# A hybrid decoder trunk: the output matrix w_out by seven half products, the first of them placed inside the output projection

## The chip, the core and the metric

The kernel runs on one core of one Trainium2 chip. The core has five engines that work side by side and meet at semaphores: TensorE (PE in the profile; PEld is its loading of the stationary operand), VectorE (DVE), ScalarE (ACT), GpSimd (POOL) and SyncE (SP), which here issues the transfers between the chip's main memory and the on-chip memory. TensorE writes its sums to banks of a separate memory (PSUM), from which VectorE and ScalarE read them. The metric is the device time of one execution in microseconds (us); the time of a kernel is the median of its runs.

## What is computed

Two layers of a decoder trunk over 512 tokens of width 1024, in float32. Each layer runs three mixers on the normed input, gates and merges them, projects the merge with `w_out`, and adds a feed-forward part:

```python
    xn = rmsnorm(x, norm1_g)
    proj = xn @ w_in
    ...
    y_ssd = ssd_mixer(...)
    y_mla = mla_mixer(...)
    y_gdn = gdn_mixer(...)
    gates = jax.nn.sigmoid(gate_logits.astype(jnp.float32)).astype(x.dtype)
    g_ssd, g_mla, g_gdn = jnp.split(gates, N_BRANCH, axis=-1)
    mixed = g_ssd * (y_ssd @ w_ssd_out) + g_mla * (y_mla @ w_mla_out) + g_gdn * (y_gdn @ w_gdn_out)
    h = x + mixed @ w_out
    f = jnp.square(jax.nn.relu(rmsnorm(h, norm2_g) @ w_up)) @ w_down
    return h + f
```

`w_ssd_out`, `w_mla_out`, `w_gdn_out` and `w_out` are 1024 x 1024, `w_up` is 1024 x 4096, `w_down` 4096 x 1024.

## The kernel before

**Float32 from three products.** Each operand of a large matmul is split into a rounded part "hi" and a remainder "lo" (`split_half`, lines 149 to 156: a copy on ScalarE at line 154, a subtraction on VectorE at line 155). `mm3` (lines 180 to 184) then issues three matmuls into one bank: hi·hi, hi·lo, lo·hi. Weights come in by SP as raw panels of 512 KB into two buffers `wraw` (line 161) and are split 512 columns at a time into a ring of four pairs `whi`, `wlo`. There are four accumulator banks ("acc"), three small ones ("sm") and one for transposes ("yt").

**Order of the work.** The program is written as straight Python; a scheduler places each instruction in its engine's queue by the program's order, its priority (`tc.high_priority()` moves instructions ahead) and its own estimate of when the inputs are there. On the chip each queue runs in the order that was so fixed. A pool is a stretch of on-chip memory whose tags each have one or more buffers ("slots"); a tile waits until the tile before it in the slot is released, and, for a pool opened where another was closed, until the tiles that lay at the same place are released (`reuse_waits="tile"`).

**Around the change.** The mixers live in the pool `br`, whose first tag is "tok" (five slots of 8 KB, among them v and the gate z of the two DeltaNet units). Each layer ends its mixers with two `gdn_unit` calls, which have a recurrent chain over four token blocks, and then `out_proj(w_gdn_out, 2, ...)` (lines 459 to 473), the projection of the third branch. It has four steps `dp`; each takes 256 of the 1024 output columns: 48 matmuls for two tiles of gate logits (from `xh`, `xl`, the normed input), a tanh on ScalarE into two "cva" buffers (line 464), then 48 matmuls with the branch's matrix, and on VectorE the multiplication by the gate (line 472) and the addition to the branches before (line 473), into eight tiles `mixed[d]`, one for each 128 columns, transposed so that columns lie on partitions and the 512 tokens along the row. (The gate's sigmoid is a tanh, so `mixed` holds twice the merge; the factor 0.5 comes later.)

Then `br` is closed, the residual h (4 tiles of 128 tokens, 2 MB) is loaded (line 1101), the eight `mixed` tiles are split to hi and lo (lines 250 and 251), and `w_out` runs as two column halves of 512 (`dense_T`): for each of the four token groups, all eight k, three matmuls of 128 x 128 by 512. The evacuation at line 1115 adds half the result to h, and ScalarE squares h for the norm (line 271). In the second half the token groups run one after the other; after the third, `norm_half(0)` scales tokens 0 to 255 by their norm (line 285), transposes them on TensorE (line 290) and splits them to `xh`, `xl` with the gain (lines 254 and 255), eight rows of 256 tokens. The other half of the tokens follows inside the first panel of `w_up`.

**The feed-forward part** takes four quarters `qd` of 1024 columns. `up` makes four panels of 256 columns of relu squared; after each panel it loads a block of `w_down` (`after(c)`, line 1201, 1024 KB each, in the order b11, b12, b22, b21), and after the third and fourth sums p1 = b11 + b12 and p3 = b12 + b22 on VectorE (line 1195). `down` multiplies by seven half products instead of eight (a Strassen form): the token halves, the row halves and the column halves make 2 x 2 blocks on each side, and seven products of sums of blocks (a11, a12, s2, s1, s3, s4, a22 with b11, b21, p2, p1, p3, b22, p4) give the four result blocks. Each product is 2 token groups x 4 k x 3 = 24 matmuls of 512 columns; VectorE adds each result to h (line 1236), makes p2 = p1 + b22 (line 1251) and p4 = p2 + b21 (line 1264). In the last quarter of layer 0 the norm of tokens 0 to 255 for layer 1 stands ahead of the last product a22, whose four k are then run token group by token group.

Of the kernel before, what the change touches and what calls it, by code (L numbers as in the profile page):

```python
# [10 lines left out]
F32 = mybir.dt.float32  # L11
# [44 lines left out]
def hybrid_kernel(ctx, tc, a, out, depth=2, taps=None):  # L56
# [294 lines left out]
    for ly in range(depth):  # L351
# [107 lines left out]
        def out_proj(w2d, br, yh, yl, pl, part=range(4), after=None):  # L459
            for dp in part:  # L460
                tg = []
                for ps in dense_F(weights(w_in, O_GATE + br * D + dp * 256, 256, D), tiles(256), D, xh, xl, after=after):
                    t_ = mk(pl, [P, S], F32, "cva", 2)
                    act.activation(t_, ps, AF.Tanh, scale=0.5)
                    tg.append(t_)
                for j, ps in enumerate(dense_F(weights(w2d, dp * 256, 256, D), tiles(256), D, yh, yl, after=after)):
                    d = 2 * dp + j
                    if mixed[d] is None:
                        mixed[d] = mk(lp, [P, S], F32, "mix", 8)
                        dve.scalar_tensor_tensor(mixed[d], tg[j], 1.0, ps, ALU.add, ALU.mult)  # L470
                    else:
                        dve.scalar_tensor_tensor(tg[j], tg[j], 1.0, ps, ALU.add, ALU.mult)
                        dve.tensor_tensor(mixed[d], mixed[d], tg[j], ALU.add)
# [619 lines left out]
        out_proj(a["w_gdn_out"][ly], 2, *yg, br)  # L1093
# [5 lines left out]
        h = mk(hpl, [P, T, D], F32, "h")  # L1099
        for t in range(T):  # L1100
            sync.dma_start(h[:, t, :], xsrc[t * P : (t + 1) * P, :])
        mh, mlo = hilo_tags(lp, "y")
        for d in range(KD):
            split_act(mh[d], mlo[d], mixed[d])
        last = ly == depth - 1
        hts = [h[:, t] for t in range(T)]
        ssq = [mk(sp, [P, 2], F32, "nss", 4) for _ in range(T)]
        xh, xl = hilo_tags(lp, "x")
        n2 = lambda i, pl, *tag: norm_half(i, hts, ssq, lambda k: col(g_n2 + k), pl, xh, xl, *tag)
        with tc.tile_pool(name="wo", bufs=1, reuse_waits="tile") as wo:  # L1110
            for c in range(2):

                def ev(t, ps):
                    hs_ = h[:, t, c * 512 : (c + 1) * 512]
                    dve.scalar_tensor_tensor(hs_, ps, 0.5, hs_, ALU.mult, ALU.add)
                    square(ssq[t][:, c : c + 1], hs_, wo, "hj")

                hold = list(zip(*hilo_tags(wo, "w"))) if c == 1 else None
                hook = (lambda t: t == 2 and n2(0, wo, "xr", 2)) if c == 1 else None
                dense_T(weights(a["w_out"][ly], c * 512, 512, D, hold), 512, D, mh, mlo, ev, hook=hook)  # L1120
# [16 lines left out]
        with tc.tile_pool(name="ff", bufs=1, reuse_waits="tile") as fp:  # L1137
# [51 lines left out]
            def down_weights(qd):  # L1189

                b = {}

                def plus(o, x, y):
                    for q in (slice(0, 1024), slice(1024, 2048)):
                        dve.tensor_tensor(o[:, q], x[:, q], y[:, q], ALU.add)

                def after(c):
                    i, j = ((0, 0), (0, 1), (1, 1), (1, 0))[c]
                    b[i, j] = mk(fp, [P, 4 * 512], F32, f"wr{i}{j}")
                    rows, cols = (slice(o + 512 * e, o + 512 * (e + 1)) for o, e in ((qd * D, i), (0, j)))  # L1200
                    sync.dma_start(b[i, j].rearrange("p (k n) -> p k n", k=4), a["w_down"][ly][rows, cols].rearrange("(k p) n -> p k n", p=P))
# [6 lines left out]
                return b, after  # L1208

            def down(qd, ops, b):  # L1210

                x, z = ([acc_bank() for _ in range(2)] for _ in range(2))

                def product(ps, n, raw, start, i, j, op, done):  # L1220

                    w = []
                    for k in range(4):
                        w.append(split_half(raw(k)))
                        if done == 2 and qd == 3:
                            continue
                        for t in range(2):
                            mul(ps, n, w, k, t, start)
                    for t in range(2):
                        if done == 2 and qd == 3:  # L1230
                            for k in range(4):
                                mul(ps, n, w, k, t, start)
                        r = 2 * i + t
                        hs_ = h[:, r, j * 512 : (j + 1) * 512]
                        with tc.high_priority():
                            dve.tensor_tensor(hs_, hs_, ps[t], op)  # L1236
                        if done and qd == 3:
                            square(h_ssq[r][:, j : j + 1], hs_, fp, "fs", 3)
                            if done == 2:
                                finish(r, gb)  # L1240

                def mul(ps, n, w, k, t, start):
                    ah, al = (o[:, k % 2 * 256 + t * P : k % 2 * 256 + (t + 1) * P] for o in ops[n][k // 2])
                    mm3(ps[t], ah, al, *w[k], start and k == 0, k == 3, not start)

                b11, p3, b21, b22, p1 = (b[n] for n in ((0, 0), (0, 1), (1, 0), (1, 1), "p1"))

                halves = [mk(fp, [P, 2 * S], F32, "f", 4) for _ in range(2)]
                for q, o in enumerate(halves):
                    cs = slice(q * 1024, (q + 1) * 1024)  # L1250
                    dve.tensor_tensor(o, p1[:, cs], b22[:, cs], ALU.add)
                gb = None
                if last and qd == 3:
                    gb = mk(fp, [P, D], F32, "f", 4)
                    sync.dma_start(gb, a["final_norm_g"].partition_broadcast(P))
                p2 = lambda k: halves[k // 2][:, k % 2 * 512 : k % 2 * 512 + 512]
                of = lambda o: lambda k: o[:, k * 512 : (k + 1) * 512]
                product(x, "a11", of(b11), True, 0, 0, ALU.add, 0)
                product([sm_bank() for _ in range(2)], "a12", of(b21), True, 0, 0, ALU.add, 1)
                p4 = p1  # L1260

                def plus4(q):
                    cs = slice(q * 1024, (q + 1) * 1024)
                    dve.tensor_tensor(p4[:, cs], halves[q], b21[:, cs], ALU.add)

                product(x, "s2", p2, False, 0, 1, ALU.subtract, 0)
                product(z, "s1", of(p1), True, 1, 1, ALU.add, 0)
                plus4(0)
                product(x, "s3", of(p3), False, 1, 1, ALU.subtract, 1)
                plus4(1)  # L1270
                product(z, "s4", of(b22), False, 0, 1, ALU.add, 1)
                if qd == 3:
                    for t in range(2):
                        finish(t, gb)
# [51 lines left out]
```

## Time and profile before

| | |
|---|---|
| median of 3 runs | 2317.55 us (2316.7 to 2318.01) |
| the profiled execution | 2320.83 us, span 2319.1 us |
| mean granted TensorE clock | 0.996 of full speed |
| matmuls | 11858 |
| `w_out` in layer 0 | 785.4 to 830.75 us of the span |
| the four steps of the third projection, layer 0 | to 785.4 us |
| first quarter of `w_down`, layer 0 | within 874 to 913 us |

The profile is one execution. Times in its rows are us from the span's start; "L155" is line 155 of the kernel before, and an arrow "out<-in" names the tile written and the tiles read. A row of the timeline has the start, the length, engine and line, and in square brackets how long the engine was idle before it and what released it. Matmuls are pipelined: one that is listed with 0.39 us does not keep the next from starting 0.23 us after it. In the rows by stretch, the columns are the stretch, its length, the busy time and count of PE, PEld, DVE, ACT and POOL, the granted clock, the share of the 16 transfer engines and GB/s.

### The profile page before, as it was taken

Reading aid. Unit: us, or ns where it says so; the run is one execution under the profiler, and the core shown is the slowest. Engines: PE = TensorE matmul, PEld = TensorE weight load, DVE = VectorE, ACT = ScalarE, POOL = GpSimd, SP = SyncE. Lnnn points to the kernel's source line nnn. Section 1 sums busy time; section 2 is a strip of 40 time slices with the busy share of each in tenths; the row PEclk is TensorE's granted clock in tenths of the full one; section 3 lists DMA queues with packets and bytes.
Section 4 is the critical chain, followed back from the end, with each engine's and each line's share of the span. In section 5 each row is a group of like instructions: output and inputs, shape, how many; then the busy total and the mean of one; then the engine's idle time right before and its main releaser. Section 6 shows DMA issues by size and latency. Waiting matters only on the chain.

```text
span 2319.1 us, 32185 instructions
## 1 busy us (share of the span) xinstructions
PE 2283.2 (98%) x11858; PEld 1877.5 (81%) x11858; DVE 1590.1 (69%) x3132; ACT 1177.4 (51%) x2445; POOL 59.0 (3%) x74
## 2 busy tenths in 40 slices
PE   8999999999999999999999999999999999999998
PEld 7788787878887888888888877878788878888886
DVE  7777566866665558767867775668657645678668
ACT  6766744333443445554657666443334434545545
POOL 0000000000000000000000000000000000000000
PEclk9999999999999999999999999999999999999999
DMA  4223634442322443233132236334422224333231
GB/s 141 80 73 100 192 100 118 134 130 73 87 69 73 152 140 108 82 110 118 51 97 79 70 110 192 98 112 143 119 82 83 64 82 154 128 118 100 91 109 46
DMA packets 220158, 244.15 MB, mean 105 GB/s; under 512 B 34384, under 2 KB 172512, under 8 KB 220000
## 3 DMA queue, kind: packets, MB, share of 16 engines
q1 hardware_dynamic: 220000, 242.09, 34.4%
q8 instruction: 93, 1.52, 0.3%
q14 instruction: 65, 0.53, 0.1%
HBM read 225.60 MB, written 11.74 MB: 102 GB/s over the span
## 4 chain that ended last, share of the span: by engine, by line
PE 89%; DVE 6%; ACT 1%; DMA 1%; POOL 1%; issue 1%; SPq 0%; DVEq 0%; POOLq 0%; ACTq 0%
PE acc L182 23%; PE acc L183 23%; PE acc L184 23%; PE sm L182 2%; PE sm L183 2%; PE sm L184 2%; DVE wlo L155 1%; PE sm L751 1%; DVE tok L879 1%; PE sm L649 1%; DVE gQ L878 1%; PE sm L1036 1%; POOL gms L259 1%; ACT whi L154 1%; PE sm L760 1%
## 5 line engine op out<-in xcount | busy, mean ns | idle before, releaser
L155 DVE TENSOR_TENSOR wlo<-wraw,whi 128x512 fp32r<-128x512 f32 (+1 forms) x552 | 377.3, 687 | 406.0 <-ACT whi L154 399.1
L154 ACT CAST whi<-wraw 128x512 fp32r<-128x512 f32 (+1 forms) x552 | 340.3, 618 | 595.0 <-PE acc L183 414.6
L184 PE MATMUL acc<-xh,wlo 128*128 128x512 f32 (+1 forms) x1376 | 536.4, 390 | 0.0
L182 PE MATMUL acc<-xh,whi 128*128 128x512 f32 (+1 forms) x1376 | 535.7, 390 | 0.0
L183 PE MATMUL acc<-xl,whi 128*128 128x512 f32 (+1 forms) x1376 | 534.9, 389 | 0.0
L184 PEld LDWEIGHTS acc<-xh,wlo 128*128 128x128 f32 x1376 | 259.6, 189 | 49.4
L183 PEld LDWEIGHTS acc<-xl,whi 128*128 128x128 f32 x1376 | 259.6, 189 | 49.1 <-DVE xl L255 0.4
L182 PEld LDWEIGHTS acc<-xh,whi 128*128 128x128 f32 x1376 | 259.1, 189 | 49.4 <-ACT xh L254 0.4
L183 PE MATMUL acc<-yl,whi 128*128 128x512 f32 x384 | 151.4, 394 | 0.0
L182 PE MATMUL acc<-yh,whi 128*128 128x512 f32 x384 | 150.8, 396 | 0.0
L184 PE MATMUL acc<-yh,wlo 128*128 128x512 f32 x384 | 150.0, 391 | 0.0
L690 DVE SCALAR_TENSOR_TENSOR ckl<-acc,pc,ckl 128x511 f32<-128x511 f32 (+2 forms) x168 | 120.4, 743 | 15.4 <-ACT ckl L686 8.1
L154 ACT CAST whi<-wr 128x512 fp32r<-128x512 f32 x128 | 79.5, 621 | 66.6 <-PE acc L184 28.1
L184 PE MATMUL acc<-whi,yl 128*128 128x512 f32 x256 | 99.7, 389 | 0.0
L182 PE MATMUL acc<-whi,yh 128*128 128x512 f32 x256 | 99.7, 389 | 0.0
L183 PE MATMUL acc<-wlo,yh 128*128 128x512 f32 x256 | 99.6, 389 | 0.0
L155 DVE TENSOR_TENSOR wlo<-wr,whi 128x512 fp32r<-128x512 f32 x128 | 86.0, 686 | 12.1 <-ACT whi L154 11.4
L182 PEld LDWEIGHTS acc<-yh,whi 128*128 128x128 f32 x384 | 71.6, 188 | 16.1 <-ACT yh L254 1.7
L184 PEld LDWEIGHTS acc<-yh,wlo 128*128 128x128 f32 x384 | 72.2, 188 | 14.5
L183 PEld LDWEIGHTS acc<-yl,whi 128*128 128x128 f32 x384 | 72.2, 188 | 13.9
L454 ACT ACTIVATE eE<-eE,cum 128x128 f32<-128x128 f32 x192 | 63.2, 391 | 23.4 <-DMA eE<-d_c 23.4
L1236 DVE TENSOR_TENSOR h<-h,acc 128x512 f32<-128x512 f32 x96 | 61.6, 681 | 0.0
(429 smaller groups left out, 4418.3 us busy)
## 6 DMA issues: line engine op xcount, KB each, us to landing
wraw<-in_w_in_dram SPq DMA_DIRECT2D x144, 512.0 KB, 3.6
wraw<-in_w_up_dram SPq DMA_DIRECT2D x64, 512.0 KB, 3.6
wr<-in_w_down_dram SPq DMA_DIRECT2D x32, 1024.0 KB, 5.1
eE<-d_c SPq DMA_DIRECT2D x48, 256.0 KB, 4.1
wraw<-in_w_mla_out_dram SPq DMA_DIRECT2D x16, 512.0 KB, 3.3
eE<-d_e SPq DMA_DIRECT2D x32, 256.0 KB, 3.2
wraw<-in_w_ssd_out_dram SPq DMA_DIRECT2D x16, 512.0 KB, 3.4
wraw<-in_w_gdn_out_dram SPq DMA_DIRECT2D x16, 512.0 KB, 3.3
```

The lines of the kernel that those rows point to most:

```text
L154: act.copy(hi, raw)
L155: dve.tensor_tensor(lo, raw, f32(hi), ALU.subtract)
L182: pe.matmul(o, ah, bh, start=start, stop=False, skip_group_check=more)
L183: pe.matmul(o, ah, bl, start=False, stop=False, skip_group_check=more)
L184: pe.matmul(o, al, bh, start=False, stop=stop, skip_group_check=more)
L259: pool.tensor_tensor(o, o, (exp if exp is not None else nhalf)[:, : o.shape[1]], ALU.pow)
L454: act.activation(o[:, i], o[:, i], AF.Relu, scale=-1.0, bias=cum[:, t, h0 + i : h0 + i + 1])
L649: pe.transpose(ps[:, n : n + P], pn[t][:, kb * P : (kb + 1) * P], ident)
L690: dve.scalar_tensor_tensor(acc[:, d:], ps[:, : S - d], taps_[3 - d], acc[:, d:], ALU.mult, ALU.add)
L751: pe.matmul(py[64 * i : 64 * i + 64, c * P : (c + 1) * P], xd[:, t, h * 64 : (h + 1) * 64], e2[h // 4][:, h % 4, :], start=True, stop=True)
L760: pe.matmul(po[:, c * P : (c + 1) * P], st[:, c * P : (c + 1) * P], ctl[:, tok], start=True, stop=True)
L1236: dve.tensor_tensor(hs_, hs_, ps[t], op)
```

## The change

`w_out` is computed in the seven-product form of `down`. For that the functions inside the feed-forward part become `seven_weights` and `seven`, used by both. For `w_out`:

- `br` is closed ahead of the third projection. The pools for h and for `w_out` ("wo") open there, and the gates of the projection's steps go to slots of these pools: steps 0 to 2 to the slots that the blocks of `w_out`, their sum p1 and h take afterwards, step 3 to two "fs" buffers.
- After steps 0 to 2, h and the four blocks of `w_out` are loaded, in the order b11, b21, b12, b22 (1024 KB each, in place of eight panels of 512 KB through `wraw`).
- The first product, a11, stands ahead of step 3, which uses small banks for its gates. The other six follow step 3.
- The operands are made from `mixed` in 256-token pieces, d by d: `put` scales by 0.5 on ScalarE and subtracts on VectorE, `comb` adds or subtracts two pieces on VectorE. They take the "ck" tiles, a tag "s3", and, once step 3's gates have read the normed input, the sixteen `xh`, `xl` tiles.
- The norm of tokens 0 to 255 stands ahead of a22, as in the last quarter of `down`.
- In both uses p1 is summed after the second block is asked for (before: after the third) and p3 after the third (before: after the fourth).

```diff
-        def out_proj(w2d, br, yh, yl, pl, part=range(4), after=None):
+        def out_proj(w2d, br, yh, yl, pl, part=range(4), after=None, make=None, gate_banks=lambda: None):
...
-                for ps in dense_F(weights(w_in, O_GATE + br * D + dp * 256, 256, D), tiles(256), D, xh, xl, after=after):
-                    t_ = mk(pl, [P, S], F32, "cva", 2)
+                for j, ps in enumerate(dense_F(weights(w_in, O_GATE + br * D + dp * 256, 256, D), tiles(256), D, xh, xl, None, gate_banks(), after)):
+                    t_ = make(dp, j) if make else mk(pl, [P, S], F32, "cva", 2)
...
-                        dve.scalar_tensor_tensor(tg[j], tg[j], 1.0, ps, ALU.add, ALU.mult)
-                        dve.tensor_tensor(mixed[d], mixed[d], tg[j], ALU.add)
+                        with tc.high_priority() if make else nullcontext():
+                            dve.scalar_tensor_tensor(tg[j], tg[j], 1.0, ps, ALU.add, ALU.mult)
+                            dve.tensor_tensor(mixed[d], mixed[d], tg[j], ALU.add)
...
-        out_proj(a["w_gdn_out"][ly], 2, *yg, br)
         bp.close()
...
-        mh, mlo = hilo_tags(lp, "y")
-        for d in range(KD):
-            split_act(mh[d], mlo[d], mixed[d])
...
+        def seven_weights(pl, w2d, r0):
...
+            def after(c):
+                i, j = ((0, 0), (0, 1), (1, 1), (1, 0))[c]
+                b[i, j] = mk(pl, [P, 4 * 512], F32, f"wr{i}{j}")
...
+                if c == 1:
+                    b["p1"] = mk(pl, [P, 4 * 512], F32, "wp1")
+                    plus(b["p1"], b[0, 0], b[0, 1])
+                if c == 2:
+                    plus(b[0, 1], b[0, 1], b[1, 1])
...
+        def seven(pl, ops, b, sq=None, before_last=None, fin=None, nf=4, pre=None, mid=None):
+            x, z = ([acc_bank() for _ in range(2)] for _ in range(2))
+            def product(ps, n, raw, start, i, j, op, done):
+                w = []
+                if pre:
+                    pre(n)
+                for k in range(4):
+                    w.append(split_half(raw(k)))
+                    if done == 2 and sq:
+                        continue
+                    for t in range(2):
+                        mul(ps, n, w, k, t, start)
+                for t in range(2):
+                    if done == 2 and sq:
+                        for k in range(4):
+                            mul(ps, n, w, k, t, start)
...
+                    with tc.high_priority():
+                        dve.tensor_tensor(hs_, hs_, ps[t], op)
+                    if done and sq:
+                        square(sq[r][:, j : j + 1], hs_, pl, "fs", 3 if nf == 4 else 2)
...
+            product(x, "a11", of(b11), True, 0, 0, ALU.add, 0)
+            if mid:
+                mid()
+            product([sm_bank() for _ in range(2)], "a12", of(b21), True, 0, 0, ALU.add, 1)
+            p4 = mk(pl, [P, 4 * 512], F32, "wr00") if mid else p1
...
+            product(x, "s2", p2, False, 0, 1, ALU.subtract, 0)
+            product(z, "s1", of(p1), True, 1, 1, ALU.add, 0)
+            plus4(0)
+            product(x, "s3", of(p3), False, 1, 1, ALU.subtract, 1)
+            plus4(1)
+            product(z, "s4", of(b22), False, 0, 1, ALU.add, 1)
+            if before_last:
+                before_last()
+            product(x, "a22", of(p4), False, 1, 0, ALU.add, 2)
 
         with tc.tile_pool(name="wo", bufs=1, reuse_waits="tile") as wo:
-            for c in range(2):
...
-                dense_T(weights(a["w_out"][ly], c * 512, 512, D, hold), 512, D, mh, mlo, ev, hook=hook)
+            slots = {(0, 0): (wo, "wr00"), (0, 1): (hpl, "h"), (1, 0): (wo, "wr10"), (1, 1): (wo, "wp1"),
+                     (2, 0): (wo, "wr01"), (2, 1): (wo, "wr11"), (3, 0): (wo, "fs"), (3, 1): (wo, "fs")}
...
+            out_proj(a["w_gdn_out"][ly], 2, *yg, wo, (0, 1, 2), make=gate_tile)
+            h = mk(hpl, [P, T, D], F32, "h")
+            for t in range(T):
+                sync.dma_start(h[:, t, :], xsrc[t * P : (t + 1) * P, :])
...
+            b, after = seven_weights(wo, a["w_out"][ly], 0)
+            for c in (0, 3, 1, 2):
+                after(c)
...
+            ops["a11"], ops["s3"] = ck_pair(), list(zip(*hilo_tags(wo, "s3", 2)))
+
+            def mid():
+                out_proj(a["w_gdn_out"][ly], 2, *yg, wo, (3,), make=gate_tile, gate_banks=lambda: [sm_bank() for _ in range(2)])
+                fh, fl = hilo_tags(lp, "x")
+                for i, n in enumerate(("a12", "s2", "s1", "s4")):
+                    ops[n] = [(fh[2 * i + e], fl[2 * i + e]) for e in range(2)]
+                ops["a22"] = ck_pair()
+
+            def put(n, d, s):
+                hi, lo = (x[:, d % 2 * 256 : d % 2 * 256 + 256] for x in ops[n][d // 2])
+                act.mul(hi, s, 0.5)
+                dve.scalar_tensor_tensor(lo, s, 0.5, f32(hi), ALU.mult, ALU.subtract)
+
+            def comb(x, y, op):
+                s = mk(wo, [P, 256], F32, "fc", 8)
+                dve.tensor_tensor(s, x, y, op)
+                return s
...
+            def forms(n):
+                for d in range(4):
+                    with tc.high_priority() if d > 1 and n in ("a12", "s2") else nullcontext():
+                        form(n, d)
+
+            def form(n, d):
+                if n == "a11":
+                    put("a11", d, t0(d))
+                    put("s3", d, comb(t0(d), t1(d), ALU.subtract))
+                if n == "a12":
+                    put("a12", d, t0(d + 4))
+                if n == "s2":
+                    s = comb(t1(d), t1(d + 4), ALU.subtract)
+                    s2 = comb(s, t0(d), ALU.subtract)
+                    put("s2", d, s2)
+                    held.append((s, s2))
+                if n == "s1":
+                    s, s2 = held[d]
+                    put("s1", d, s)
+                    put("s4", d, comb(t0(d + 4), s2, ALU.add))
+                if n == "a22":
+                    put("a22", d, t1(d + 4))
...
+            seven(wo, ops, b, ssq, lambda: n2(0, wo, "f", 2), nf=2, pre=forms, mid=mid)
...
-                if c == 2:
-                    b["p1"] = mk(fp, [P, 4 * 512], F32, "wp1")
-                    plus(b["p1"], b[0, 0], b[0, 1])
-                if c == 3:
-                    plus(b[0, 1], b[0, 1], b[1, 1])
...
+                return seven_weights(fp, a["w_down"][ly], qd * D)
...
-                down(qd, ops, b)
+                seven(fp, ops, b, *ends(qd))
```

More of the change, by code (lines that the diff above doesn't have):

```diff
@@ L1109, in hybrid_kernel, with plus @@
[L1109 to L1120 removed]
+        def seven_weights(pl, w2d, r0):
+            b = {}
+            def plus(o, x, y):
+                for q in (slice(0, 1024), slice(1024, 2048)):
+                    dve.tensor_tensor(o[:, q], x[:, q], y[:, q], ALU.add)
+            def after(c):
+                i, j = ((0, 0), (0, 1), (1, 1), (1, 0))[c]
+                b[i, j] = mk(pl, [P, 4 * 512], F32, f"wr{i}{j}")
+                rows, cols = (slice(o + 512 * e, o + 512 * (e + 1)) for o, e in ((r0, i), (0, j)))
+                sync.dma_start(b[i, j].rearrange("p (k n) -> p k n", k=4), w2d[rows, cols].rearrange("(k p) n -> p k n", p=P))
+                if c == 1:
[3 more added lines that the diff above has]
+                    plus(b[0, 1], b[0, 1], b[1, 1])
+            return b, after
@@ L1208, in down_weights @@
[L1208 to L1251, printed above, removed]
@@ L1258, in down @@
[L1258 to L1268, printed above, removed]
```

63 lines of the change are left out of this document (40 added, 23 removed).

## The prediction

> **What bounds the kernel now.** I read the page's busy line, then the list of what TensorE waited for, then busy times by stretch around the edit, then the order of the instructions at its edges.
>
> ```profile
> PE 2283.2 (98%) x11858; PEld 1877.5 (81%) x11858; DVE 1590.1 (69%) x3132; ACT 1177.4 (51%) x2445; POOL 59.0 (3%) x74
> ...
> PE sm L1017 <- DVE tok L1014: 3.5, 8, 0.5
> PE sm L912 <- DMA wk<-d_x: 3.1, 2, 1.9
> PE yt L1067 <- DVE tok L1062: 2.9, 4, 0.9
> ```
>
> TensorE is busy 98%. Its longest waits come from the recurrent chain of the DeltaNet units, a few us in all, and none from the output projection or from `w_out`. The stretches (us, busy and count for PE, PEld, DVE, ACT and POOL, granted clock, DMA share, GB/s) say the same. They are the fourth projection step, `w_out` with the start of `w_up`, and the first `w_down`, all of layer 0:
>
> ```profile
> 763.60:785.40 21.80, 21.80 (x97) 18.03 (x97) 11.21 (x19) 9.23 (x17) 0.00 (x0) 1.00 0.31 96
> ...
> 785.40:830.75 45.35, 45.35 (x210) 37.62 (x208) 24.55 (x45) 18.90 (x41) 1.67 (x3) 1.00 0.45 151
> ...
> 836.50:842.30 5.80, 5.67 (x46) 5.13 (x45) 4.66 (x9) 3.10 (x8) 0.00 (x0) 1.00 1.05 410
> ...
> 874.00:913.00 39.00, 39.00 (x173) 32.14 (x172) 34.96 (x54) 21.38 (x36) 0.00 (x0) 1.00 0.31 108
> ```
>
> TensorE never pauses in `w_out`, so a matmul taken away there is time taken away, as long as the other engines keep up. VectorE is busy 24.55 of 45.35 us there. In the last row, a stage with the very scheme that the change brings to `w_out`, VectorE is busy 34.96 of 39.00 us and TensorE still does not wait. These rows decide my forecast.
>
> **What is removed.** `w_out` runs from the first of these rows to the start of `w_up` in the last:
>
> ```profile
> 785.41 0.39 PE L182 MATMUL acc<-whi,yh 128*128 128x512 f32 x1
> ...
> 795.38 0.39 PE L184 MATMUL acc<-whi,yl 128*128 128x512 f32 x1
> ...
> 830.52 0.39 PE L184 MATMUL acc<-wh,yl 128*128 128x512 f32 x1
> 830.75 0.28 PE L182 MATMUL acc<-xh,whi 128*128 128x256 f32 x1
> ...
> 836.50 1.47 PE L290 MATMUL sm<-ct,f 128*128 128x128 f32 x12
> ```
>
> Between the first two lie 44 steps, so a matmul costs 9.97/44 = 0.2266 us. The stage has 2 column halves x 4 token groups x 8 k x 3 = 192 of them (43.5 us; 16 transposes make up the 45.34). Seven products of 2 x 4 x 3 = 24 are 168. So 24 x 0.2266 = **5.44 us a layer, 10.88 in two layers**, go for certain. All else is whether new waits give it back. The eight updates of h at L1115 and the eight splits of the mixed rows (L250, L251) go too; they delayed nothing.
>
> **What is added, mostly on VectorE.** Its prices:
>
> ```profile
> 785.39 0.69 DVE L473 TENSOR_TENSOR mix<-mix,cva 128x512 f32<-128x512 f32 x1
> ...
> 786.00 0.68 DVE L472 SCALAR_TENSOR_TENSOR cva<-cva,acc 128x512 f32<-128x512 f32 x1
> ...
> 786.60 0.68 DVE L155 TENSOR_TENSOR wlo<-wraw,whi 128x512 fp32r<-128x512 f32 x1
> ...
> 1142.22 1.22 DVE L1264 TENSOR_TENSOR wp<-f,wr 128x1024 f32<-128x1024 f32 x1
> ...
> 1143.36 1.44 DVE L155 TENSOR_TENSOR wlo<-wr,whi 128x512 fp32r<-128x512 f32 x2
> ...
> L779 DVE TENSOR_TENSOR wk<-wk 128x256 f32<-128x256 f32 x16 | 6.7, 420 | 2.9 <-ACT wk L778 2.9
> ```
>
> Back to back, a 512-wide operation steps 0.605 us (0.08 less than its length) and a 1024-wide one 1.14. The new 256-wide ones are not in the trace as such; the nearest row takes 0.42, so they step between 0.34 and 0.42, and I take 0.34 because they stand back to back.
>
> Call T the end of the fourth projection step. After T come six products, 144 matmuls or 32.6 us. In that time VectorE owes: the last tile's mixing, 2 x 0.605 = 1.2; 21 weight splits, 12.7; ten updates of h, 6.05; for rows d = 2 and 3, fourteen 256-wide operations of a12, s2, s1 and s4, 4.8; four of a22, 1.4; plus4, 2.3; the scaling for the norm, 2.0. That is **30.4 of 32.6 us**, 93%, against 90% in the stage that does not stall. It holds only if 11.6 us more are done before T: the sums p1, p3 and p2 (6 x 1.14 = 6.8) and the fourteen operations for d = 0 and 1 (4.8). The fourth step leaves VectorE 21.8 - 11.2 = 10.6 us, the a11 product 5.4 less four splits and two updates (3.6), 12.4 together. So it fits, just. The forms of a11 and s3 (12 x 0.34 = 4.1) need only steps 0 and 1 and go into step 2, which is as loose. ScalarE adds about 12 splits and 28 short scalings over the whole, and at 18.90 of 45.35 it has room.
>
> **The junction at T.** a12 needs the last mixing for k = 2 and 3. Its k = 0 and 1 are 12 matmuls, 2.7 us, and k = 2 another 1.36, which gives 4.1 us until k = 3. The last tile needs two VectorE steps (1.2), a ScalarE scaling and a subtraction of some 0.4 each, and about 0.2 of latency: 2.2 us. It is covered; uncovered it would cost those 2.2. For junction and dense middle I take 0.5 us a layer. The bounds are 0 (as in `w_down`) and 9.4 (30.4 + 11.6 - 32.6, nothing done early).
>
> **The tail.** Before, the norm of tokens 0 to 255 was hidden under two token groups of 5.4 us; now only a22 hides it. The trace has this arrangement once, where layer 0's last a22 precedes layer 1:
>
> ```profile
> 1155.49 0.39 PE L182 MATMUL acc<-whi,yh 128*128 128x512 f32 x1
> ...
> 1159.32 0.55 PE L290 MATMUL sm<-ct,f 128*128 128x128 f32 x3 [0.50 <-DVE f L285]
> ...
> 1163.01 0.32 PE L182 MATMUL acc<-mix,xh 128*128 128x352 f32 x1
> ...
> 1165.31 0.63 PE L290 MATMUL sm<-ct,f 128*128 128x128 f32 x4 [0.53 <-DVE xl L255]
> ...
> 1161.97 1.26 DVE L255 SCALAR_TENSOR_TENSOR xl<-sm,pc,xh 128x256 fp32r<-128x256 f32 x3
> ...
> 1168.72 0.47 DVE L255 SCALAR_TENSOR_TENSOR xl<-sm,pc,xh 128x256 fp32r<-128x256 f32 x1
> ```
>
> It waits 0.50 + 0.53 = 1.03 us. Behind `w_out` it is tighter: `w_up`'s first half takes 830.75 to 836.50, 5.75 us, where layer 1's front takes 48 x 0.16 = 7.7, and a22 holds all four split buffers, so `w_up`'s four splits come late. I take 1.5 us a layer. The lower bound is 0.1 (5.80 - 5.67 in the row of 836.50), the upper 4: VectorE's eight gains end 13.7 us after a22's start (1169.2 - 1155.5), against 12.9 for a22, 16 transposes and the half (5.44 + 1.7 + 5.75), and the second half-norm could be as late again and a little more.
>
> **What moves, at no cost.** The gates of steps 0 to 2 go to separate slots, so bp.close comes ahead of the projection. By tag order and size wr10 and wp1 lie over the 8 KB "tok" tiles that hold v and z of DeltaNet unit 1. Step 1's gates therefore wait for the unit's end, not for a cva buffer:
>
> ```profile
> 725.59 0.69 ACT L254 ACTIVATE yh<-yt,pc 128x512 fp32r<-128x512 f32 x1 [1.09 <-PE yt L1067]
> ...
> 730.58 0.60 ACT L464 ACTIVATE cva<-acc 128x512 f32<-128x512 f32 x1 [1.70 <-DVE mix L473]
> ...
> 787.73 1.90 SPq L1101 DMA_DIRECT2D h<-in_x_dram  x4
> ...
> 830.71 2.25 SPq L1201 DMA_DIRECT2D wr<-in_w_down_dram  x4
> ...
> 879.13 28.19 SPq L1201 DMA_DIRECT2D wr<-in_w_down_dram  x4
> ...
> wr<-in_w_down_dram SPq DMA_DIRECT2D x32, 1024.0 KB, 5.1
> ```
>
> The unit ends at 725.6, before 730.58, so this is not later. On SP the four h loads go ahead of step 3, and eight `w_out` loads become four of 1024 KB (5.1 us to land). The loads of b12 and b22 wait for step 2's mixing, and step 3's panels stand behind them in SP's queue; the a11 product (5.4 us) and a double buffer cover that. Without the cover it is up to 5.1 us a layer. In the feed-forward part p1 and p3 are summed one panel earlier, so VectorE may stand at a load with the splits behind it. From the second quarter on, the loads go out from 879 to 907, before that quarter's `w_up` starts (913), and are long there; for the first, about two panels (over 10 us) separate slot and sum. Price 0, at most 5.1 a layer.
>
> **The sum.** 5.44 - 0.5 - 1.5 = 3.44 us a layer, 6.9 in two. The profiled execution took 2320.83 us (span 2319.1), 3.3 above the median of the runs, so it would be 2313.9 and the median 2317.55 - 6.9 = **2310.6 us**.
>
> **One thing a wait can trigger.** At the start of layer 1's latent attention TensorE idles, and the clock follows:
>
> ```profile
> 1212.54 1.23 PE L491 MATMUL sm<-ct,yh 128*128 128x128 f32 x8 [1.15 <-DVE yh L486]
> ...
> 1214.00:1216.00 2.00, 2.00 (x10) 1.72 (x11) 1.41 (x4) 1.56 (x3) 1.12 (x1) 0.74 0.00 0
> 1216.00:1218.00 2.00, 2.00 (x6) 1.51 (x6) 1.06 (x3) 1.10 (x3) 0.00 (x0) 0.50 0.00 0
> ...
> 1217.07 0.63 PE L183 MATMUL acc<-ckl,whi 128*128 128x512 f32 x1
> 1217.50 0.63 PE L184 MATMUL acc<-ckh,wlo 128*128 128x512 f32 x1
> ```
>
> One wait of 1.15 us was followed by some 3 us at half clock (steps of 0.43), about 1.5 us lost; two of 0.5 at 1159 and 1165 were not. The Trainium skill, "TensorE: Matmul & The Clock Gate", "HAM oscillation — how this bites in real kernels", warns only of idle gaps above about 3.4 us; by that rule my waits would cost no clock and the sum would stay. The trace disagrees: its gap was a third of that. By the row, a tail wait in one piece costs 1.5 us more a layer, which gives 2310.6 + 3.0 = 2313.6; it is counted in rival 3.
>
> **The rivals.**
> 1. *The forecast*: TensorE bound, about 2 us of new waits a layer. For it: `w_down`'s row and the 1.03 us. Its own range is 2307.5 to 2312.9. Chance 0.50.
> 2. *Everything hidden*: 2317.55 - 10.9 = 2306.7. For it: 39.00 of 39.00 in `w_down`. Against it: the tail has less cover than before. Chance 0.12.
> 3. *The tail takes most of it*: 3 us there and 0.5 in the middle, plus 1.5 at half clock, 5.0 a layer, net 0.4: about 2316.7. For it: eight gains took 7.2 us at the layer boundary, more than `w_up`'s half of 5.75. Against it: TensorE can take both `w_up` tiles row by row as the gains come. Chance 0.16.
> 4. *Slower: VectorE becomes the bound after T.* Its queue runs in order. Where the sums and early forms are placed behind T, TensorE runs dry between s2 and s4. Slack is 32.6 - 30.4 = 2.2 us, so with the tail's 1.5 it decides once 2.2 + 5.4 - 1.5 = 6.1 of the 11.6 us slide. With all of them, 9.4 + 1.5 - 5.4 = 5.5 a layer are lost: 2328.5. For it: only 0.8 us to spare before T (12.4 against 11.6). Against it: `w_down`. Chance 0.17, of which 0.05 slide only so far that the time stays within 0.2%.
> 5. *The change doesn't do what it says*: the gates give their slots up too late for the loads. a11 stands ahead of step 3 in TensorE's order, so a late b11 stops both. At half a load, 2.55 us a layer, it is 2310.6 + 5.1 = 2315.7. Against it: b11 takes the slot of step 0, two steps (43 us) ahead. Chance 0.05.
>
> Faster by over 0.2% (below 2312.9; 0.2%, 4.6 us, is what this measurement can tell from no change) is cases 1 and 2 and a little of 3: 0.63. Within: most of 3, all of 5 and the mild part of 4, 0.25. Slower 0.12. The range goes from the full gain, 2306.5, to 2318.5, where rival 3 and the mild part of 4 end.
>
> **What would show it.** Right: 168 matmuls of 0.227 us a layer in `w_out`, granted clock 1.00, TensorE idle about 2 us between step 3 and `w_up`'s second panel, most of it before transposes at L290 or `w_up`'s first matmuls. VectorE should be 90% busy or more from T to a22. Rival 4 would show as TensorE waiting for VectorE's 256-wide forms or splits in s2, s1 or s4; rival 3 as waits above 2 us at the norm or a clock below 1; rival 5 as a split of b11 that waits for its load. I am wrong if any other stage moves by more than 1 us, above all the DeltaNet unit 1 or `w_up`'s second panel, where p1 now stands.

## The result, and the profile after

The changed kernel takes **2331.27 us** (median of 4 runs, 2330.94 to 2332.37); the kernel before, on the same chip, takes 2317.12. The ratio is 1.0064, with a 95% interval of 1.0047 to 1.0081: **14.2 us slower**, where 6.9 us faster was forecast. The profiled execution took 2332.37 us (span 2330.6).

On the page of the changed kernel the busy line comes first:

```profile
PE 2280.6 (98%) x11810; PEld 1873.1 (80%) x11810; DVE 1647.8 (71%) x3256; ACT 1201.1 (52%) x2509; POOL 59.5 (3%) x74
```

From its view of waits, the first and the third of TensorE's (us in total, times, longest):

```profile
PE yt L1068 <- DVE tok L1063: 9.2, 4, 4.1
...
PE sm L1037 <- issue: 3.0, 2, 1.5
```

48 matmuls are gone, 24 a layer, as counted. But the first wait, for "tok" in the recurrent chain of a DeltaNet unit, went from 2.9 us to 9.2, and the other, by "issue" (idle time for which the profile shows no cause), 1.5 us a layer, was not among the first ones. Neither stands in `w_out`. The busy times by stretch (us; busy and count for PE, PEld, DVE, ACT and POOL; granted clock; DMA share; GB/s) place them. First the kernel before, unit 1 of layer 0 and the same place in layer 1:

```profile
700.00:720.00 20.00, 18.66 (x96) 14.92 (x94) 13.07 (x41) 7.84 (x27) 2.02 (x2) 1.00 0.19 54
...
1860.00:1880.00 20.00, 19.05 (x93) 14.92 (x92) 10.95 (x25) 8.12 (x19) 1.01 (x1) 1.00 0.24 65
```

Then the changed kernel, with the stretches of `w_out` between:

```profile
700.00:720.00 20.00, 13.23 (x67) 10.47 (x67) 11.37 (x39) 6.58 (x24) 2.01 (x2) 0.91 0.12 42
720.00:740.00 20.00, 20.00 (x86) 16.08 (x85) 10.85 (x19) 8.73 (x16) 0.00 (x0) 0.92 0.47 158
...
780.00:800.00 20.00, 20.00 (x90) 16.59 (x89) 17.28 (x28) 8.72 (x18) 0.00 (x0) 1.00 0.25 77
800.00:820.00 20.00, 20.00 (x89) 16.19 (x88) 19.59 (x41) 12.77 (x28) 0.00 (x0) 1.00 0.00 1
820.00:840.00 20.00, 18.15 (x104) 15.08 (x102) 16.66 (x36) 12.22 (x29) 2.48 (x4) 1.00 0.28 96
...
1860.00:1880.00 20.00, 13.41 (x49) 9.81 (x50) 8.88 (x24) 6.32 (x17) 1.01 (x1) 0.66 0.08 26
```

From 680 to 700 the two still agree (TensorE busy 19.06 us and 19.07). From 700 to 720, still in DeltaNet unit 1, TensorE idles 20 - 13.23 = 6.77 us, against 1.34 before, and the granted clock drops to 0.91 and 0.92. Layer 1 repeats it (6.59 us against 0.95, clock 0.66). In `w_out` VectorE is busy 19.59 of 20 us and TensorE 20.00 of 20.00: full, and not waiting.

What stood in those 6.77 us? The groups of accumulator matmuls in the window from 675 us to the unit's end (count; shortest, median and longest in ns; first and last start) show it. Before, one of the three kinds of the gates' products (tokens "xh" and "xl"):

```profile
L183 PE MATMUL acc<-xl,whi x27: 387/395/483, 676.6 to 722.3; 128*128 128x512 f32 x27
```

After:

```profile
L183 PE MATMUL acc<-xl,whi x16: 389/392/477, 675.3 to 695.1; 128*128 128x512 f32 x16
```

Before, the gates go on to 722.3; after, they stop at 695.1. Sixteen a kind, 48 in all, are the gates of step 0. The kernel before starts 82 by the unit's end (28, 27 and 27 of the three kinds): those 48 and 34 of step 1's. They fill the gaps of unit 1's chain, and the change leaves them out of there. The lists of ScalarE's instructions say why. Before, step 0's first tanh comes as soon as its bank is full:

```profile
695.49 0.60 ACT L464 ACTIVATE cva<-acc 128x512 f32<-128x512 f32 x1 [1.45 <-PE acc L184]
```

After, it comes 30 us later, without idle time before it, right behind the unit's last evacuation:

```profile
724.89 0.69 ACT L254 ACTIVATE yh<-yt,pc 128x512 fp32r<-128x512 f32 x1 [0.56 <-PE yt L1068]
725.47 0.59 ACT L464 ACTIVATE wr<-acc 128x512 f32<-128x512 f32 x1
725.95 0.60 ACT L464 ACTIVATE h<-acc 128x512 f32<-128x512 f32 x1
```

Until a tanh has read its bank, step 0's gates hold two of the four accumulator banks, and its product with the branch's matrix (`acc<-yh,whi`) takes the others, so step 1's gates have none. The trace doesn't show who holds a bank; the experiments below test whether the late tanh is the cause. What TensorE does meanwhile:

```profile
707.97 0.47 PE L184 MATMUL acc<-yh,wlo 128*128 128x512 f32 x1
709.94 1.13 PE L1037 MATMUL sm<-wk,eE 128*128 128x128 f32 x8 [1.50 <-issue]
...
716.03 0.33 PE L1068 MATMUL yt<-ct,tok 128*128 128x128 f32 x1 [4.09 <-DVE tok L1063]
717.13 1.22 PE L182 MATMUL acc<-yh,whi 128*128 128x512 f32 x2 [0.78 <-ACT yh L254]
...
719.86 0.63 PE L183 MATMUL acc<-yl,whi 128*128 128x512 f32 x1
720.29 0.63 PE L184 MATMUL acc<-yh,wlo 128*128 128x512 f32 x1
...
726.20 0.42 PE L182 MATMUL acc<-xh,whi 128*128 128x512 f32 x1
```

Three waits (1.50, 4.09, 0.78), then steps of 0.43 us instead of 0.23, which is half clock. At 726.20, behind the tanh, the gates of step 1 begin.

**The account of layer 0.** Times of the two traces can't be subtracted as they stand, because they are not in step when unit 1 begins. The same row of ScalarE, before and after:

```profile
688.63 1.14 ACT L1024 ACTIVATE wk<-sm,gcd 128x128 f32<-128x128 f32 x4 [2.43 <-DVE wk L1019]
```

```profile
687.27 1.14 ACT L1025 ACTIVATE wk<-sm,gcd 128x128 f32<-128x128 f32 x4 [2.42 <-DVE wk L1020]
```

The changed kernel is 1.36 us ahead here, from a stage that the change doesn't touch (from 500 to 520 us its granted clock was 0.91, against 0.83 before). Counted from this row, the unit's last evacuation comes 0.66 us later (724.89 against 725.59, plus the lead of 1.36), and 34 matmuls x 0.2266 = 7.7 us are pushed behind it: 8.4 us are lost. The first feed-forward evacuation, which both kernels have, measures the sum. Before and after:

```profile
845.60 0.60 ACT L1172 ACTIVATE f<-acc 128x512 f32<-128x512 f32 x1 [0.91 <-PE acc L184]
```

```profile
850.41 0.60 ACT L1307 ACTIVATE f<-acc 128x512 f32<-128x512 f32 x1 [0.86 <-PE acc L184]
```

It is 4.81 us late, 6.17 counted from the row above. -5.44 + 8.4 leaves 3.2 for the tail of `w_out`.

### The profile page after: what moved, and what is told of

It reads as the page before. It is cut to its first block, busy times and chain, and to the rows that moved or that the text cites. A ratio compares the mean times of both kernels' runs of the same rounds, so it can differ in the third digit from the quotient of the medians.

```text
span 2330.6 us, 32281 instructions
## 1 busy us (share of the span) xinstructions
PE 2280.6 (98%) x11810; PEld 1873.1 (80%) x11810; DVE 1647.8 (71%) x3256; ACT 1201.1 (52%) x2509; POOL 59.5 (3%) x74
## 4 chain that ended last, share of the span: by engine, by line
PE 87%; DVE 7%; ACT 2%; issue 1%; POOL 1%; DMA 1%; SPq 0%; DVEq 0%; POOLq 0%; ACTq 0%
PE acc L182 22%; PE acc L183 22%; PE acc L184 22%; PE sm L184 2%; PE sm L182 2%; PE sm L183 2%; DVE wlo L155 2%; PE sm L752 1%; DVE tok L880 1%; ACT whi L154 1%; PE sm L650 1%; DVE gQ L879 1%; PE sm L1037 1%; POOL gms L259 1%; PE sm L761 1%
## 5 line engine op out<-in xcount | busy, mean ns | idle before, releaser
L155 DVE TENSOR_TENSOR wlo<-wraw,whi 128x512 fp32r<-128x512 f32 (+1 forms) x536 | 366.1, 686 | 363.5 <-ACT whi L154 358.0
L182 PE MATMUL acc<-xh,whi 128*128 128x512 f32 (+1 forms) x1344 | 522.7, 390 | 0.7 <-ACT xh L254 0.7
L184 PE MATMUL acc<-xh,wlo 128*128 128x512 f32 (+1 forms) x1344 | 523.1, 390 | 0.0
L183 PE MATMUL acc<-xl,whi 128*128 128x512 f32 (+1 forms) x1344 | 522.8, 389 | 0.3 <-DVE xl L255 0.3
L154 ACT CAST whi<-wr 128x512 fp32r<-128x512 f32 x168 | 104.4, 621 | 111.0 <-PE acc L183 50.1
L155 DVE TENSOR_TENSOR wlo<-wr,whi 128x512 fp32r<-128x512 f32 x168 | 113.5, 687 | 33.9 <-ACT whi L154 33.1
L182 PEld LDWEIGHTS acc<-yh,whi 128*128 128x128 f32 x384 | 72.9, 191 | 17.3 <-ACT yh L254 2.6
L183 PE MATMUL acc<-wlo,xh 128*128 128x512 f32 (+1 forms) x208 | 80.1, 385 | 0.0
L184 PE MATMUL acc<-whi,xl 128*128 128x512 f32 (+1 forms) x208 | 79.7, 385 | 0.0
L182 PE MATMUL acc<-whi,xh 128*128 128x512 f32 (+1 forms) x208 | 79.2, 382 | 0.0
L1144 DVE TENSOR_TENSOR h<-h,acc 128x512 f32<-128x512 f32 x120 | 77.2, 681 | 0.2 <-PE acc L184 0.2
```

Source lines behind the costliest of these rows:

```text
L154: act.copy(hi, raw)
L155: dve.tensor_tensor(lo, raw, f32(hi), ALU.subtract)
L182: pe.matmul(o, ah, bh, start=start, stop=False, skip_group_check=more)
L183: pe.matmul(o, ah, bl, start=False, stop=False, skip_group_check=more)
L184: pe.matmul(o, al, bh, start=False, stop=stop, skip_group_check=more)
```

## The experiments

Theory A: the tanh of step 0 is late because its tile lies in a pool that opens behind unit 1, and ScalarE's queue has it behind the unit's last release; TensorE loses the matmuls that filled the gaps of unit 1's chain. Theory B: the new `w_out` costs the time, by VectorE's load, its tail or the loads. Ratios are against the kernel before on the same chip, with 95% intervals.

**e1: step 0 ahead of the pool's close again**, in the mixer's pool, the rest as changed (but step 0's mixing, without `make`, has no raised priority).

```
+        out_proj(a["w_gdn_out"][ly], 2, *yg, br, (0,))
         bp.close()
...
-            slots = {(0, 0): (wo, "wr00"), (0, 1): (hpl, "h"), (1, 0): (wo, "wr10"), (1, 1): (wo, "wp1"),
+            slots = {(1, 0): (wo, "wr10"), (1, 1): (wo, "wp1"),
...
-            out_proj(a["w_gdn_out"][ly], 2, *yg, wo, (0, 1, 2), make=gate_tile)
+            out_proj(a["w_gdn_out"][ly], 2, *yg, wo, (1, 2), make=gate_tile)
```

> The changed kernel, but step 0 of the projection keeps its gates in the mixers' pool, which is closed after step 0 instead of ahead of it. Theory A (no tile of a newly opened pool is placed before the closed pool's last tile is released, so step 0's two gate tiles hold two accumulator banks until DeltaNet unit 1 ends, and step 1's 48 gate matmuls, 10.9 us, no longer fill its chain): step 0's gates leave the banks about 25 us before the unit's end, as before the change, and the time is 2317.1 - 10.9 + 2 x 2.0 for the tail = 2310, within 2. Theory B (the loss comes from the seven products themselves: their loads, their priorities or the mixing placed ahead disturb the chain): it stays within 3 of 2331.

2315.0 us (11 runs), ratio 0.9993 (0.9983 to 1.0002). Of the 14.2 us nothing is left. Its first tanh of step 0, and its stretch:

```profile
693.71 0.60 ACT L464 ACTIVATE cva<-acc 128x512 f32<-128x512 f32 x1 [1.45 <-PE acc L184]
```

```profile
700.00:720.00 20.00, 18.62 (x97) 14.95 (x96) 12.79 (x41) 7.31 (x25) 2.01 (x2) 1.00 0.16 51
```

The tanh is back at 693.71 (this trace is 1.78 us ahead of the one of before in unit 1) and TensorE at 18.62 of 20. Theory A holds for the loss in unit 1; the time still lies 5 us above what it expected.

**e2: the moved pool alone**, with the old `w_out`.

```
-        out_proj(a["w_gdn_out"][ly], 2, *yg, br)
         bp.close()
...
+        gp = ExitStack()
+        wg = gp.enter_context(tc.tile_pool(name="wg", bufs=1, reuse_waits="tile"))
+        out_proj(a["w_gdn_out"][ly], 2, *yg, wg)
+        gp.close()
```

> The kernel before, with nothing changed but that the mixers' pool is closed ahead of the third projection, whose two gate buffers then lie in a new pool; w_out as before. Theory A: step 0's gates wait for the end of unit 1, and the time rises by what the changed kernel lost beside its gain, 14.2 + 10.9 - 4.0 = 21 us, to 2338, at least to 2330. Theory B: no change, 2317 within 2.

2335.81 us, ratio 1.0083 (1.0064 to 1.0103), **19.4 us slower** without one seven-product matmul. The stretch, ScalarE's list and the queue of SP:

```profile
700.00:720.00 20.00, 13.24 (x68) 10.17 (x67) 11.68 (x39) 6.70 (x25) 2.01 (x2) 0.93 0.37 132
```

```profile
726.22 0.69 ACT L254 ACTIVATE yh<-yt,pc 128x512 fp32r<-128x512 f32 x1 [0.90 <-PE yt L1067]
726.80 1.07 ACT L464 ACTIVATE cva<-acc 128x512 f32<-128x512 f32 x2
```

```profile
710.87 1.45 SPq L1104 DMA_DIRECT2D h<-in_x_dram  x3
```

The same late tanh and 13.24 of 20. The last row adds something: the loads of h, into another pool opened behind the close, start at 710.87, some 15 us before the unit's last release. So not everything in the new pools is held until the old one is empty. What holds the tanh is either its place in ScalarE's queue or its address; e5 separates the two.

**e5: the same, at the old addresses.** Is it memory that comes free late? An unused tile shifts the gates of e2 to the very addresses that they have in the kernel before.

```
+        mk(wg, [P, 13824], F32, "pad")
         out_proj(a["w_gdn_out"][ly], 2, *yg, wg)
```

> As the second experiment (the kernel before, pool closed ahead of the projection), but an unused tile pushes the two gate buffers in the new pool to the very addresses that they had in the mixers' pool, where nothing of unit 1 lies. Theory A in its sharper form (the order of ScalarE's queue is fixed with every use of a new pool behind the closed pool's last release; no semaphore on the chip is involved): no help, step 0's gates still follow unit 1's last evacuation directly, 2336 within 2. Theory D (the chip waits for the tile that lay at the same address): step 0's gates come at about 695 as before, 2317 within 2.

2333.53 us, ratio 1.0071 (1.0058 to 1.0084), half a microsecond below theory A's range and far from theory D's. The tanh is as late as in e2, where the kernel before writes the same addresses at 695.49:

```profile
726.65 0.69 ACT L254 ACTIVATE yh<-yt,pc 128x512 fp32r<-128x512 f32 x1 [0.90 <-PE yt L1067]
727.24 1.08 ACT L464 ACTIVATE cva<-acc 128x512 f32<-128x512 f32 x2
```

So it isn't the address. In the trace the tanh has no semaphore of its own to wait for there; it only stands behind L254 in ScalarE's queue. The Trainium skill, "Perfetto Trace Analysis", "Tensor Engine Instruction (MATMUL, LD_WEIGHTS)", says that "ACT/DVE/GPSIMD are strict FIFO"; these rows agree.

**e3: the seven products alone**, with all gates ahead of the close.

```
+        out_proj(a["w_gdn_out"][ly], 2, *yg, br)
         bp.close()
...
-            out_proj(a["w_gdn_out"][ly], 2, *yg, wo, (0, 1, 2), make=gate_tile)
...
-                out_proj(a["w_gdn_out"][ly], 2, *yg, wo, (3,), make=gate_tile, gate_banks=lambda: [sm_bank() for _ in range(2)])
```

> The seven products without the slots: the whole projection stays in the mixers' pool, then h and the blocks are loaded, and a11 stands behind step 3. Theory A: the chain of unit 1 is as before the change, but the first block comes only after the last mixing, so TensorE idles about 2.2 + 5.1 + 1.2 = 8.5 us a layer, with half clock behind it 10: 2317.1 - 10.9 + 4 + 2 x 8.5 to 10 = 2327 to 2330. Theory B: the chain loses its cover here too, over 2340.

2357.32 us, ratio 1.0178 (1.0161 to 1.0194): far above theory A's 2327 to 2330, which is missed. It is in theory B's range (over 2340), but not for theory B's reason: unit 1 keeps its cover here (from 700 to 720 TensorE is busy 18.67 of 20 us), which speaks for theory A once more. The stretches around the start of `w_out`, SP's queue, the issues with their median time to landing, and the rows of ScalarE and TensorE that end the wait:

```profile
780.00:790.00 10.00, 1.60 (x8) 0.99 (x6) 9.64 (x25) 4.65 (x13) 0.00 (x0) 0.79 1.05 406
790.00:800.00 10.00, 5.14 (x12) 3.80 (x13) 7.80 (x19) 5.04 (x11) 0.00 (x0) 0.52 0.05 17
```

```profile
772.38 2.08 SPq L1193 DMA_DIRECT2D h<-in_x_dram  x4
774.50 6.39 SPq L1114 DMA_DIRECT2D wr<-in_w_out_dram  x4
...
wr<-in_w_out_dram SPq DMA_DIRECT2D x4, 1024.0 KB, 10.5
...
794.21 2.16 ACT L154 CAST whi<-wr 128x512 fp32r<-128x512 f32 x4
...
794.86 0.80 PE L182 MATMUL acc<-whi,ckh 128*128 128x512 f32 x1 [13.26 <-ACT whi L154]
```

With the pool behind the whole projection, h and all four blocks are asked for in 8.5 us (772.4 to 780.9), the DMA engines are full (share 1.05), and TensorE stands for 13.26 us and then works at half clock (0.52). The loads are the smaller part of this. The first block, asked for at 774.50, is there at about 785 by the median of 10.5 us (an estimate), but ScalarE makes its first split only at 794.21, without idle time before it: the splits stand behind the small forms of the other products, with which VectorE is busy 9.64 of 10 us from 780 to 790. So most of the wait, some 9 of 13 us, is the order of the queues behind a busy VectorE, close to what rival 4 feared, and the expectation had no term for it. In the changed kernel the first of these loads go out at 735 (h) and 749 (the first block), during the projection, a11 stands ahead of step 3, and TensorE waits for nothing between 770 and 800. e3 therefore doesn't show the price of the loads alone; it shows that the whole projection can't simply go ahead of the close with the rest left as it is.

**e4: the block sums one panel later in the feed-forward part**, as they were before.

```
-                if c == 1:
+                if c == 1 + late:
...
-                if c == 2:
+                if c == 2 + late:
...
-                return seven_weights(fp, a["w_down"][ly], qd * D)
+                return seven_weights(fp, a["w_down"][ly], qd * D, 1)
```

> The changed kernel, but in w_down the sums p1 and p3 stand one panel later again, as before the change. If the earlier sums cost nothing (the prediction's price), 2331 within 1.5 under theories A and B alike. If VectorE stands at loads there (theory C), it is faster by 3 us or more.

2333.69 us, ratio 1.0072 (1.0055 to 1.0089): no better than the changed kernel, and 1.2 us above the range that was expected. The earlier sums cost nothing that could be seen.

**e7: the kernel of e1 again**, beside e5 and e6.

> The first experiment once more, beside the one with the held splits: 2315 within 2.

2315.04 us (11 runs), ratio 0.9993 (0.9985 to 1.0002): the same as e1.

**e6: e1 with a22's four splits in tiles of their own**, so that `w_up`'s splits needn't wait for a22's matmuls.

```
-                    w.append(split_half(raw(k)))
+                    w.append(split_half(raw(k), hold()[k] if hold and done == 2 else None))
...
+            def hold():
+                if not kept:
+                    r = mk(wo, [P, 4 * 512], F32R, "wr01")
+                    hs, ls = hilo_tags(wo, "s3", 2)
...
```

> The first experiment (step 0's gates in the mixers' pool), and the four weight splits of a22 get buffers of their own (the operands of s3 and the block of p3, both free by then) instead of the ring of four that the first panel of w_up needs next. If the tail's loss of about 3 us a layer, seen in the first experiment's starts, comes from w_up's splits being made among the eight gains on VectorE, it falls by 1 to 2 us a layer, 2 to 4 below the run without it. If the chain of the norm itself sets it, no change.

2311.43 us (8 runs), ratio **0.9977** (0.9966 to 0.9988), 4.9 us faster than the kernel before: it beats both. The stretch of the tail, first e1, then e6:

```profile
820.00:840.00 20.00, 18.11 (x130) 16.19 (x131) 15.90 (x33) 11.05 (x26) 1.42 (x3) 1.00 0.72 263
```

```profile
820.00:840.00 20.00, 19.28 (x140) 17.21 (x139) 14.78 (x34) 9.73 (x23) 2.48 (x4) 1.00 0.66 238
```

TensorE's listed idle time falls from 1.89 to 0.72 us a layer, and the median by 3.6 us from e1's and e7's (2315.0). So the tail was real, and the split buffers made about half of it.

## Why the prediction was wrong, by its own steps

**What is removed: held.** 48 matmuls are gone at 0.2266 us each, 10.9 us.

**The junction and the dense middle: 0, where 0.5 a layer was taken.** TensorE works 20.00 of 20.00 us from 780 to 820, with VectorE at 17.28 and 19.59. That VectorE would be near its limit was right, and it was harmless. Rival 4's 2328.5 lies near the measured time, but its mechanism did not occur in the changed kernel: TensorE never waits for a form or a split in s2, s1 or s4.

**The tail: mis-sized, 1.5 taken, 3.2 measured.** Its place was right, and 3.2 lies within its bounds of 0.1 and 4. The changed kernel's TensorE list there:

```profile
828.29 0.39 PE L183 MATMUL acc<-wlo,ckh 128*128 128x512 f32 x1
829.12 0.55 PE L290 MATMUL sm<-ct,f 128*128 128x128 f32 x3 [0.44 <-DVE f L285]
...
833.41 0.28 PE L184 MATMUL acc<-xh,wlo 128*128 128x256 f32 x1
834.06 0.50 PE L182 MATMUL acc<-xh,whi 128*128 128x256 f32 x2 [0.37 <-ACT xh L254]
835.45 0.63 PE L290 MATMUL sm<-ct,f 128*128 128x128 f32 x4 [0.88 <-DVE xl L255]
```

The listed waits are 0.44 + 0.37 + 0.88 = 1.69 us. From start to start, less the step of what stands between (0.227 for 512 columns, 0.12 for 256), the same three cost 0.60, 0.53 and 1.15, 2.28 together, since a matmul's modelled end lies well behind the time at which the next could have started. The other 0.9 of the account's 3.2 isn't traced to single rows. The prediction had read the 1.03 us of the layer boundary in the listed way, and so its model for the tail was too small from the start. VectorE's list shows the cause:

```profile
831.02 1.30 DVE L155 TENSOR_TENSOR wlo<-wraw,whi 128x512 fp32r<-128x512 f32 x2 [0.16 <-ACT whi L154]
832.23 0.87 DVE L255 SCALAR_TENSOR_TENSOR xl<-sm,pc,xh 128x256 fp32r<-128x256 f32 x2
...
833.62 1.29 DVE L155 TENSOR_TENSOR wlo<-wraw,whi 128x512 fp32r<-128x512 f32 x2
834.83 1.26 DVE L255 SCALAR_TENSOR_TENSOR xl<-sm,pc,xh 128x256 fp32r<-128x256 f32 x3
```

`w_up`'s splits, held back until a22 frees their buffers, stand between the gains that the norm waits for; e6 frees them earlier and gains.

**"What moves, at no cost": this is the step that failed.** It priced the gates' move by memory alone: which tiles lie under step 1's slots, and when they come free (725.6 against 730.58). Both were true and neither decided. It asked nothing about step 0's gates, and nothing about ScalarE's queue, where the close ahead of the projection puts step 0's tanh behind the unit's last evacuation. (That the close does it, e1 and e2 show; why the scheduler orders it so was not looked into.) And it didn't ask who holds the accumulators meanwhile. The runs: 19.4 us for this move alone (e2), 17.2 at the old addresses (e5), gone when step 0 goes back (e1). 730.58 was the row to read differently: it is a late gate, but TensorE had done most of step 1's gate matmuls before the unit's end, because the tanh at 695.49 had freed a bank. The prediction's own last sentence named the sign: "any other stage moves by more than 1 us, above all the DeltaNet unit 1".

**The loads and the earlier sums: held.** TensorE waits for no load of `w_out`, and p1 and p3 cost nothing that could be seen (e4). Asked for together, as in e3, the blocks take 10.5 us to land and not the 5.1 that the prediction took for the case without cover.

**A stage that the prediction did not look at: the last quarter of layer 1.** Every kernel here with the shared `seven` has a new wait of 1.29 us there; the kernel before and e2 and e5, which keep the old functions, have none. e4 has it too, so it doesn't come from the earlier sums. In e1, of ScalarE and TensorE:

```profile
2278.45 1.14 ACT L154 CAST whi<-f 128x512 fp32r<-128x512 f32 x2 [1.45 <-DVE f L1160]
...
2279.12 0.74 PE L182 MATMUL acc<-whi,mix 128*128 128x512 f32 x2 [1.29 <-ACT whi L154]
```

A weight split waits for a half of p2, which VectorE makes later in this quarter than the kernel before does. From start to start it costs 1.8 us. No run isolates why the queue's order differs.

**"One thing a wait can trigger": right in kind, in another place.** Half clock came in the chain of unit 1, not in the tail.

**The sum.** Whole executions differ by where the clock happened to fall, also in stages that no edit touches. So each stage is measured between two rows that both kernels have: from unit 1 to the first feed-forward evacuation in each layer, with the rows of the account of layer 0, and over the last quarter of layer 1. The figures are in us against the kernel before:

| run | layer 0 | layer 1 | last quarter | together | medians, with 95% interval |
|---|---|---|---|---|---|
| changed | 6.2 | 7.3 | 1.8 | 15.3 | 14.2 (10.9 to 18.8) |
| e2, the move alone | 8.6 | 8.4 | 0.0 | 17.0 | 19.4 (14.8 to 23.9) |
| e5, the same at the old addresses | 9.7 | 8.3 | 0.0 | 18.1 | 17.2 (13.4 to 19.5) |
| e4, the sums late | 5.9 | 6.2 | 1.8 | 13.9 | 17.3 (12.7 to 20.6) |
| e1, step 0 back | -2.2 | -2.2 | 1.8 | -2.6 | -1.4 (-3.9 to 0.5) |
| e7, e1 again | -2.2 | -2.2 | 1.8 | -2.7 | -1.3 (-3.5 to 0.5) |
| e6, e1 with held splits | -3.8 | -3.9 | 1.7 | -6.0 | -4.9 (-7.9 to -2.8) |

The forecast's terms, each with what was measured for it, then give -10.9 for the matmuls, +17.0 for the move (e2), +2 x 3.2 for the tail and +1.8 for the last quarter: +14.3, where the medians say +14.2. Agreement to 0.1 is luck, as the intervals are several us wide. Without the move the same terms give -2.7 for e1 and e7. e6 lowers the tail from 3.2 to 1.6 a layer.

**Open.** All seven sums lie within the intervals of the medians, and nothing beyond them can be told from these runs. The 1.1 to 1.4 us by which the medians of e1, e7 and e6 lie above their sums, the 2.4 of e2 and the 3.4 of e4 are not explained.

## What to carry to other kernels

Before a pool is closed earlier in the program, list what each engine's queue will hold behind the close, and which of TensorE's banks those instructions release: one evacuation that comes late can take away matmuls that filled the gaps of another stage. A free address says when a tile may be written, not where its writer stands in the queue; read both. Where a stage has new waits, size them from start to start, because listed idle time leaves out part of it. And compare two traces between rows that both have, at both ends of a stage, because they are rarely in step where the stage begins.

## What the runs showed of the hardware that was not expected

The clock fell after short waits again, and the length of a wait did not decide it. In layer 0 TensorE worked at full speed behind the wait of 1.50 us and at half behind that of 4.09. In layer 1 it slowed already between the two:

```profile
1862.56 1.37 PE L1037 MATMUL sm<-wk,eE 128*128 128x128 f32 x8 [1.50 <-issue]
1863.71 1.92 PE L1042 MATMUL sm<-st,ft 128*128 128x256 f32 x4
1869.72 0.48 PE L1068 MATMUL yt<-ct,tok 128*128 128x128 f32 x1 [4.09 <-DVE tok L1063]
```

The same eight matmuls take 1.13 us in layer 0 (709.94) and 1.37 here, behind the same wait of 1.50. Nor is the row that the prediction read, the wait of 1.15 us at the start of layer 1's latent attention, always followed by half clock. It stands in all nine traces of this case at 1.15 or 1.16 us. In four (before, e1, e3, e7) the granted clock over the 5 us that follow is 0.66; in the other five it is 1.00. So a wait of this length can cost the clock and need not. No run tells whether the wait itself counts or all the idle time around it. The Trainium skill, "TensorE: Matmul & The Clock Gate", "HAM oscillation — how this bites in real kernels", warns of idle gaps above about 3.4 us; the 4.09 us agree with it, the 1.50 here and the 1.15 of the kernel before do not, if each wait is taken by itself.
